# A hybrid retention and attention layer: tiles turned in 32x32 blocks on VectorE instead of on TensorE

## The chip, the cores and the metric

The kernel runs on one core of one Trainium2 chip. The metric is the device time of one execution, in microseconds (us). One core has TensorE (PE, with its weight loads as PEld), VectorE (DVE), ScalarE (ACT), GpSimd (POOL) and SyncE (SP, which here only issues transfers), and 16 DMA engines between DRAM and the on-chip memories.

## The reference

The layer takes x of 1024 tokens by 2048 features in float32, normalizes it, projects it to 6656 columns, runs two groups of heads, gates them, and projects back:

```python
h = rms_norm(x, norm_w)
rq, rk, rv, rg, aq, ak, av, ag = split(h @ w_in)
# group A: 8 retention heads x 128, chunks of 128 tokens, forward and backward
q, k = rotary(rq), rotary(rk) * 128**-0.5
inner = ((q @ k.T) * decay) @ v                 # inside a chunk
kv_chunk = k.T @ (k_dec * v)                    # one 128x128 state update per chunk and direction
cross = (q * q_dec) @ prev_state                # prev_state: scan over chunks, state * chunk_decay + kv_chunk
y = inner + cross                               # both directions added
y = (y - mean(y)) * rsqrt(var(y) + eps)         # per token and head
y_ret = (y * gn_w + gn_b) * silu(rg)
# group B: 8 query heads on 2 key/value heads, window of 128 tokens, partial rotary, a sink logit
y_att = windowed_softmax_attention(aq, ak, av, sink) * silu(ag)
x = x + concat(y_ret, y_att) @ w_out
return rms_norm(x, final_norm_w)
```

## The kernel before

The big products (x by w_in, and the gated outputs by w_out) are done in float32 precision as three passes each: an operand is split into a high and a low part (`split`, L84 and L87), and `mm3` (L98 to L100) issues high x high, high x low and low x high, each a 128x128 weight against 512 columns. Blocks of 2x2 tiles are combined in Strassen's manner into seven products. A product is four program steps, a step is six of these matmuls, and a unit of seven products is 28 steps. Every projected tile (52 of them, 128 features by 1024 tokens) is stored to a DRAM tensor `pr` by SP (first contribution) or added there by a POOL transfer (L258 to L262).

Attention, retention, gating and the weight loads run beside these products as generators: `advance()` is called once per step and moves each of them to its next `yield`; `idle(n)` passes n steps. So the program is written in one order, step by step. PE, SP and POOL execute it in that order. VectorE's and ScalarE's instructions are placed by a scheduler and then executed in that order. An instruction that waits holds up everything behind it on its engine or queue.

The tiles in `pr` have features on the partitions. Some steps need tokens there:

- Attention (L557): `take_v` turns the two v tiles (`ld`) by `transposed` (L537 to L543), which puts four 128x128 transposes on PE into one PSUM bank `ax`, and then splits the bank.
- A retention head (L772): it multiplies scores (L787), turns v with two groups of four transposes and copies them out on ScalarE (L797), waits until the head before is done (`busy`), turns k in the same way (L803), scales v on ScalarE (`vd`, L808), idles three steps, and then forms the outer products of `k_tok` and `vd` on PE (L820). A scan over chunks on VectorE (L832, L834) makes the states, and each state is split at once (L84, L87) into `sH` and `sL`, 128x128 at a time. Then come the inner and the cross products (L867, L854).
- `normed` (L880): mean and variance (L882, L883), the power on POOL (L888), eight VectorE instructions per head that normalize y (L891), two groups of four PE transposes, a ScalarE instruction on each bank that applies `gn_w` and `gn_b` (L899), and the store to the DRAM tensor `mix` by SP (L905). `k_tok` and `y` share a buffer.

While one head is computed, its successor's tiles are fetched by SP: kT and qT (L738), their halves exchanged for the rotary (`rx`, L744), and vT (L761). SP also issues the weight loads `a` (L171), each of which waits for the buffer that it fills: the last use of that buffer is a VectorE product `wL` (L84). The two weight buffers' contents are made two products ahead.

Gating (L1247) reads `mix` and the gate tiles back on ScalarE's queue, applies Silu and multiplies on VectorE.

## Time and profile before

| | |
|---|---|
| median of three runs | 1526.33 us (1524.84 to 1526.47) |
| span of the profiled execution | 1524.4 us |
| that execution's time around its span | the median is 1.9 us above the span |
| PE busy | 1510.5 us, 99% of the span |
| VectorE busy | 1088.3 us, 71% |
| ScalarE busy | 686.6 us, 45% |
| POOL busy | 151.0 us, 10% |
| granted TensorE clock | 0.9 or more in every slice |
| DMA | 153,352 packets, 310.53 MB, 204 GB/s on average |
| attention | about 230 to 690 us |
| retention | about 690 to 1115 us |
| gating and output product | from about 1115 us |

A row of the grouped view reads: line, engine, operation, output<-inputs, shapes, count | busy us, mean ns of one | idle time just before, and what ended it. A row of the timeline or of the chain of waits begins with its start and its duration in us. Rows with SPq are SP's issues of transfers, not the transfers. In the rows on DMA queues stand packets, megabytes and the share of 16 engines' time.

### The profile page before, as it was taken

The page shows a single profiled execution, that of the slowest core. Times are in us where ns is not written, and L with a number is a line of the kernel's source. Part 1 is how long each engine was busy: PE and PEld are TensorE (multiplying, and loading weights), DVE is VectorE, ACT ScalarE, POOL GpSimd, SP SyncE. Part 2 cuts the span into 40 slices and gives each one's busy share as a digit, 9 for nine tenths or more (in the row PEclk, how much of TensorE's full clock was granted, in tenths as well). Part 3 has the DMA queues.
Part 4 walks back from the last instruction along what each step waited for, and adds up shares of the span by engine and source line. Part 5 has one row for each costly group of instructions (what it writes and reads, how often), then busy time and mean ns, then how long its engine had stood idle before and what let it go on. Part 6 is the DMA issues. An engine that isn't in the chain of part 4 may idle for free.

```text
span 1524.4 us, 20497 instructions
## 1 busy us (share of the span) xinstructions
PE 1510.5 (99%) x7406; PEld 1274.0 (84%) x7406; DVE 1088.3 (71%) x1943; ACT 686.6 (45%) x1139; POOL 151.0 (10%) x169
## 2 busy tenths in 40 slices
PE   9999999999999999999999999999999999999997
PEld 7888888788888888888888888888888888888886
DVE  6896594557767575756977797779755966776766
ACT  7543462234545454533445444543444643542425
POOL 0000001111010000011212000001211102020001
PEclk9999999999999999999999999999999999999999
DMA  8288847889573424796677655488689679395756
GB/s 319 68 277 316 311 166 193 222 207 251 163 204 128 138 80 167 281 315 156 139 179 205 196 174 193 152 297 299 157 207 262 152 217 251 85 212 162 219 177 251
DMA packets 153352, 310.53 MB, mean 204 GB/s; under 512 B 13697, under 2 KB 72481, under 8 KB 144418
## 3 DMA queue, kind: packets, MB, share of 16 engines
q1 hardware_dynamic: 128050, 254.15, 49.1%
q0 software_dynamic: 19728, 36.71, 15.6%
q10 hardware_dynamic: 5472, 18.36, 3.5%
q8 instruction: 58, 0.95, 0.3%
q14 instruction: 44, 0.36, 0.1%
HBM read 193.03 MB, written 124.52 MB: 208 GB/s over the span
## 4 chain that ended last, share of the span: by engine, by line
PE 84%; issue 9%; DMA 4%; DVE 2%; POOL 0%; ACT 0%; SPq 0%; ACTq 0%; POOLq 0%; DVEq 0%
PE pj L100 21%; PE pj L98 21%; PE pj L99 21%; PE ax L99 5%; PE ax L100 5%; PE ax L98 5%; PE ax L820 2%; PE ax L542 1%; DMA xt<-in_x_dram 1%; PE ax L619 1%; DMA pr<-ct 1%; PE ax L787 1%; PE ax L867 1%; DMA yt<-pr 1%; DVE wL L84 0%
## 5 line engine op out<-in xcount | busy, mean ns | idle before, releaser
L98 PE MATMUL pj<-c,wH 128*128 128x512 f32 x1444 | 576.8, 399 | 0.0
L100 PE MATMUL pj<-c,wL 128*128 128x512 f32 x1440 | 562.6, 391 | 1.6 <-DVE wL L84 1.6
L99 PE MATMUL pj<-c,wH 128*128 128x512 f32 x1444 | 563.0, 390 | 0.0
L100 PEld LDWEIGHTS pj<-c,wL 128*128 128x128 f32 x1440 | 270.3, 188 | 60.7 <-DVE wL L84 2.5
L98 PEld LDWEIGHTS pj<-c,wH 128*128 128x128 f32 x1444 | 271.6, 188 | 49.7 <-ACT ct L292 0.4
L99 PEld LDWEIGHTS pj<-c,wH 128*128 128x128 f32 x1444 | 271.8, 188 | 49.5 <-DVE c L948 0.2
L87 ACT CAST wH<-a 128x1024 fp32r<-128x1024 f32 (+1 forms) x159 | 166.3, 1046 | 250.2 <-PE pj L99 138.0
L84 DVE TENSOR_TENSOR wL<-a,wH 128x1024 fp32r<-128x1024 f32 x157 | 191.9, 1222 | 109.4 <-ACT wH L87 105.9
L292 ACT COPY ct<-pj 128x512 f32<-128x512 f32 x192 | 111.1, 584 | 220.3 <-PE pj L100 219.7
L262 POOL DMA_DIRECT2D pr<-ct x104 | 92.2, 961 | 612.9 <-DVE ct L91 474.6
L91 DVE TENSOR_TENSOR ct<-pj,ct 128x512 f32<-128x512 f32 x164 | 109.1, 688 | 58.9 <-PE pj L100 58.0
L84 DVE TENSOR_TENSOR wL<-s,wH 128x1024 fp32r<-128x1024 f32 x56 | 68.4, 1222 | 89.8 <-ACT wH L87 89.4
L99 PE MATMUL pj<-wL,c 128*128 128x512 f32 x224 | 87.3, 390 | 0.0
L100 PE MATMUL pj<-wH,c 128*128 128x512 f32 x224 | 87.2, 389 | 0.0
L98 PE MATMUL pj<-wH,c 128*128 128x512 f32 x224 | 87.1, 389 | 0.0
L99 PE MATMUL ax<-wL,c 128*128 128x512 f32 x208 | 81.2, 390 | 0.4 <-DVE wL L84 0.4
L100 PE MATMUL ax<-wH,c 128*128 128x512 f32 x208 | 80.9, 389 | 0.0
L98 PE MATMUL ax<-wH,c 128*128 128x512 f32 x208 | 80.9, 389 | 0.0
L87 ACT CAST wH<-s 128x1024 fp32r<-128x1024 f32 x56 | 59.1, 1055 | 16.4 <-PE ax L100 8.8
L87 ACT CAST sH<-st 128x128 fp32r<-128x128 f32 x112 | 29.9, 298 | 46.9 <-DVE st L834 29.2
L99 PEld LDWEIGHTS pj<-wL,c 128*128 128x128 f32 x224 | 42.0, 188 | 8.9 <-DVE wL L84 0.3
L98 PEld LDWEIGHTS pj<-wH,c 128*128 128x128 f32 x224 | 42.0, 188 | 8.8
(243 smaller groups left out, 2057.7 us busy)
## 6 DMA issues: line engine op xcount, KB each, us to landing
a<-in_w_in_dram SPq DMA_DIRECT2D x103, 512.0 KB, 5.8
kept<-c SPq DMA_DIRECT2D x28, 1024.0 KB, 7.3
c<-kept SPq DMA_DIRECT2D x28, 1024.0 KB, 9.9
pr<-ct SPq DMA_DIRECT2D x110, 256.0 KB, 5.4
pr<-ct POOLq DMA_DIRECT2D x104, 256.0 KB, 6.2
a<-in_w_out_dram SPq DMA_DIRECT2D x18, 512.0 KB, 5.4
rx<-pr SPq DMA_DIRECT2D x64, 128.0 KB, 3.8
ysrc<-mix ACTq DMA_DIRECT2D x16, 512.0 KB, 5.4
```

The source lines that it names most:

```text
L84: return nc.vector.tensor_tensor(out=dst, in0=src, in1=high.bitcast(F32), op=ALU.subtract)
L87: behind(pinned, nc.scalar.copy(out=dst_h, in_=src))
L91: nc.vector.tensor_tensor(out=dst, in0=a, in1=b, op=ALU.add)
L98: nc.tensor.matmul(po, aH, bH, start=first, stop=False, **kw)
L99: nc.tensor.matmul(po, aH, bL, start=False, stop=False, **kw)
L100: nc.tensor.matmul(po, aL, bH, start=False, stop=last, **kw)
L262: nc.gpsimd.dma_start(out=dst, in_=t, accum_op=ALU.add)
L292: nc.scalar.copy(out=t, in_=bank)
L542: nc.tensor.transpose(pt[:, blk(t)], src[:, blk(b * 4 + t)], ident)
L619: nc.tensor.transpose(pt[:, blk(j)], s[:, blk(j)], ident)
L787: nc.tensor.matmul(sc[:, blk(t)], kT[:, c], qT[:, c], start=True, stop=True)
L820: nc.tensor.matmul(p, k_tok[:, c], vd[:, c, d], start=True, stop=True)
```

## The change

PE's 208 transposes of v, k and y go. VectorE's transpose instruction turns 32x32 blocks in place: a tile of 128x512 comes out with each of its 4x16 blocks turned, but with the blocks where they were. What is left, to put block (i, j) at (j, i), is done on the way through DRAM.

- The DRAM tensors of retention's v (8), attention's v (2), the first eight `mix`, and a new `kz` (8) become `blocked`: 8 chunks of 128x128. `gather` reads such a tensor with four transfers, each to 32 partitions and 32 runs of 32 floats (128 bytes) in each; `spot` and `like` give the places for the stores, whose runs become 512 bytes. An adding POOL store of a blocked tile becomes two.
- v is gathered (attention's on SP, retention's on SP), and VectorE turns the blocks after it.
- k is turned by VectorE after its rotary into two `ct`, stored to `kz`, and gathered into `k_tok` by SP after `idle(2)`; before the outer products stands `idle(4)` in place of `idle(3)`.
- y is normalized by 64 ScalarE instructions of 128x128 (scale and bias per token; the bias is one small VectorE instruction per head), turned by VectorE into two `ct`, and stored to `mix`; gating gathers it on ScalarE's queue and applies `gn_w` and `gn_b` there, one 128x1024 instruction per tile.
- The states' split is done for both directions at once, 256 columns in place of 128, with another order inside `sH` and `sL`.

```diff
+    def gather(q, dst, src):
+        of = src.rearrange("c (b j) (a t) -> a j (c b) t", j=SQ, t=SQ)
+        for a in range(P // SQ):
+            r = slice(a * SQ, (a + 1) * SQ)
+            q(out=dst[r].rearrange("p (n t) -> p n t", t=SQ), in_=of[a])
...
             def take_v():
-                for b, pt in transposed(kv["ldv"]):
-                    split(vH[:, 4 * b:4 * b + 4], vL[:, 4 * b:4 * b + 4], chunks(pt))
+                for b in range(2):
+                    z = ct()
+                    nc.vector.transpose(out=z, in_=kv["ldv"][:, half(b)])
+                    split(vH[:, 4 * b:4 * b + 4], vL[:, 4 * b:4 * b + 4], chunks(z))
...
                     add(u, u, b)
+                    if c == T_RK:
+                        zs.append(ct())
+                        nc.vector.transpose(out=zs[i], in_=u)
                     yield
                 kq[name, h] = t
+                for i, z in enumerate(zs):
+                    yield
+                    nc.sync.dma_start(out=spot(kz[h], i), in_=chunks(z))
...
-                nc.sync.dma_start(out=t, in_=pr[T_RV + h])
+                gather(nc.sync.dma_start, t, pr[T_RV + h])
...
-                for b, pt in transposed(vs.pop(h)):
-                    nc.scalar.copy(out=v[:, 4 * b:4 * b + 4], in_=chunks(pt))
+                vT = vs.pop(h)
+                for b in range(2):
+                    nc.vector.transpose(out=v[:, 4 * b:4 * b + 4], in_=chunks(vT[:, half(b)]))
                     yield
                 while busy:
                     yield
+                yield from idle(2)
                 k_tok = ret.tile([P, NT, P], F32, name="k_tok", tag="y")
-                for b, pt in transposed(kT):
-                    nc.scalar.copy(out=k_tok[:, 4 * b:4 * b + 4], in_=chunks(pt))
-                    yield
+                gather(nc.sync.dma_start, k_tok.rearrange("p c e -> p (c e)"), kz[h])
                 start(next_of("kT", T_RK, h + 1))
...
-                yield from idle(3)
+                yield from idle(4)
...
-                        split(sH[:, 2 * to + d - 1], sL[:, 2 * to + d - 1], cur[:, d])
                         if d == 1:
+                            both = slice(i, 2 * NT - 2 - i, 2 * NT - 3 - 2 * i)
+                            split(sH[:, both], sL[:, both], cur)
...
-                for c in range(NT):
-                    nc.vector.tensor_scalar(out=y[:, c], in0=y[:, c], scalar1=mv[:, c, 0:1], scalar2=rs[:, c:c + 1],
-                                            op0=ALU.subtract, op1=ALU.mult)
-                    if c % 4 == 3:
-                        yield
+                nc.vector.scalar_tensor_tensor(out=mv[:, :, 0], in0=mv[:, :, 0], scalar=-1.0, in1=rs, op0=ALU.mult, op1=ALU.mult)
+                zs = []
+                for b in range(2):
+                    for c in range(4 * b, 4 * b + 4):
+                        nc.scalar.activation(out=y[:, c], in_=y[:, c], func=AF.Identity, scale=rs[:, c:c + 1], bias=mv[:, c, 0:1])
+                    zs.append(ct())
+                    nc.vector.transpose(out=chunks(zs[b]), in_=y[:, 4 * b:4 * b + 4])
+                    yield
+                busy.discard(h)
                 yield from idle(2)
-                outs = []
-                for b, pt in transposed(y.rearrange("p c e -> p (c e)")):
-                    yo = ct()
-                    nc.scalar.activation(out=yo, in_=pt, func=AF.Identity, scale=gw[:, h:h + 1], bias=gb[:, h:h + 1])
-                    outs.append((mix[h][:, half(b)], yo))
-                    yield
-                busy.discard(h)
-                yield
-                for dst, yo in outs:
-                    nc.sync.dma_start(out=dst, in_=yo)
+                for b, z in enumerate(zs):
+                    nc.sync.dma_start(out=spot(mix[h], b), in_=chunks(z))
...
                 nc.scalar.activation(out=g, in_=g, func=AF.Silu)
+                if t < RH:
+                    nc.scalar.activation(out=d, in_=d, func=AF.Identity, scale=gw[:, t:t + 1], bias=gb[:, t:t + 1])
                 nc.vector.tensor_tensor(out=d, in0=d, in1=g, op=ALU.mult)
...
-                        behind(True, nc.scalar.dma_start(out=d, in_=mix[t]))
+                        if t < RH:
+                            gather(lambda **kw: behind(True, nc.scalar.dma_start(**kw)), d, mix[t])
+                        else:
+                            behind(True, nc.scalar.dma_start(out=d, in_=mix[t]))
```

The order of the instructions changes with it. In the listings below a line number belongs to the kernel that the listing is of; `mm3` moves from L98 to L100 to L99 to L101, and `split`'s subtraction from L84 to L85.

On PE, at the third head's v and k. `ax<-ident,vT` and `ax<-ident,kT` are the groups of four transposes. Before:

```order
L542 MATMUL ax<-ident,vT 128x128 x4
L98 MATMUL pj<-c_5644,wH 128x512
L99 MATMUL pj<-c_5644,wH 128x512
L100 MATMUL pj<-c_5644,wL 128x512
L98 MATMUL pj<-c_5644,wH 128x512
L99 MATMUL pj<-c_5644,wH 128x512
L100 MATMUL pj<-c_5644,wL 128x512
L542 MATMUL ax<-ident,kT 128x128 x4
```

and in the changed kernel, behind the scores:

```order
L817 MATMUL ax<-qT,kT 128x128 x4
L99 MATMUL pj<-c_5650,wH 128x512
L100 MATMUL pj<-c_5650,wH 128x512
L101 MATMUL pj<-c_5650,wL 128x512
L99 MATMUL pj<-c_5650,wH 128x512
L100 MATMUL pj<-c_5650,wH 128x512
L101 MATMUL pj<-c_5650,wL 128x512
```

The groups of transposes are gone, with nothing in their place on PE; only matmuls of the projection follow the scores.

On SP, at the fourth head. `a` is a weight tile, `pr` a projected tile, `res` a piece of x for the end, `mix` the head before's output. Before:

```order
L761 DMA vT<-pr_85 128x1024
L171 DMA a_8316<-in_w_in_dram 128x4x256
L260 DMA pr_113<-ct 128x512
L260 DMA pr_114<-ct 128x512
L171 DMA a_8371<-in_w_in_dram 128x4x256
L171 DMA a_8373<-in_w_in_dram 128x4x256
L905 DMA mix_120<-ct 128x512 x2
L1153 DMA res_246<-in_x_dram 16x16384
L738 DMA kT<-pr_78 128x1024
L744 DMA rx<-pr_78 64x512 x4
L171 DMA a_8493<-in_w_in_dram 128x4x256
```

and in the changed kernel:

```order
L164 DMA vT<-pr_85 32x32x32 x4
L284 DMA pr_113<-ct 128x512
L284 DMA pr_114<-ct 128x512
L195 DMA a_8268<-in_w_in_dram 128x4x256
L195 DMA a_8270<-in_w_in_dram 128x4x256
L1180 DMA res_254<-in_x_dram 16x16384
L932 DMA mix_120<-ct 128x4x128 x2
L195 DMA a_8362<-in_w_in_dram 128x4x256
L164 DMA k_tok<-kz_137 32x32x32 x4
L762 DMA kT<-pr_78 128x1024
L768 DMA rx<-pr_78 64x512 x4
```

The gather of `k_tok` now stands on SP directly behind a weight load, `a_8362`, and ahead of the next head's kT and `rx`; the outer products on PE need it four program steps later.

On VectorE, in attention, at its first rotary. `rx` are the exchanged halves, `wL` a weight's low part, `ct` an evicted product. Before:

```order
L84 TENSOR_TENSOR wL<-s_2217,wH 128x1024
L94 TENSOR_TENSOR s_2217<-a_2073,s_2217 128x1024
L526 TENSOR_TENSOR rx_2287<-rx_2287,rt_2283 64x512
L91 TENSOR_TENSOR ct<-pj,ct 128x512 x2
L84 TENSOR_TENSOR wL<-a_2033,wH 128x1024
L526 TENSOR_TENSOR rx_2288<-rx_2288,rt_2284 64x512
```

and in the changed kernel:

```order
L85 TENSOR_TENSOR wL<-s_2227,wH 128x1024
L95 TENSOR_TENSOR s_2227<-a_2081,s_2227 128x1024
L92 TENSOR_TENSOR ct<-pj,ct 128x512 x2
L85 TENSOR_TENSOR wL<-a_2041,wH 128x1024
L85 TENSOR_TENSOR wL<-a_2079,wH 128x1024
L553 TENSOR_TENSOR rx_2302<-rx_2302,rt_2298 64x512
```

The eviction of a product and two low parts of weights now stand ahead of the rotary's product; before, they stood behind it.

More of the change, by code (lines that the diff above doesn't have):

```diff
@@ L19 @@
 P = 128
+SQ = 32
 S = 1024
@@ L136, in together, with blocked, spot, like @@
             yield
-    pr = [dram.tile([P, S], F32, name=f"pr{i}") for i in range(52)]
-    mix = [dram.tile([P, S], F32, name=f"mix{i}") for i in range(KT)]
+    BLOCKED = [*range(T_RV, T_RV + RH), T_AV, T_AV + 1]
+    def blocked(name):
+        return dram.tile([NT, P, P], F32, name=name)
+    pr = [blocked(f"pr{i}") if i in BLOCKED else dram.tile([P, S], F32, name=f"pr{i}") for i in range(52)]
+    mix = [blocked(f"mix{i}") if i < RH else dram.tile([P, S], F32, name=f"mix{i}") for i in range(KT)]
+    kz = [blocked(f"kz{i}") for i in range(RH)]
+    def spot(t, m):
+        if len(t.shape) == 2:
+            return t[:, half(m)]
+        return t[4 * m:4 * m + 4].rearrange("c p f -> p c f")
+    def like(t, ap):
+        return t if len(ap.shape) == 2 else chunks(t)
+    def gather(q, dst, src):
[3 more added lines that the diff above has]
+            q(out=dst[r].rearrange("p (n t) -> p n t", t=SQ), in_=of[a])
     rows_d = dram.tile([1, HALF], F32, name="rows_d")
@@ L259, in flush @@
             if first:
-                nc.sync.dma_start(out=dst, in_=t)
-            else:
-                nc.gpsimd.dma_start(out=dst, in_=t, accum_op=ALU.add)
+                nc.sync.dma_start(out=dst, in_=like(t, dst))
+            elif len(dst.shape) == 2:
+                nc.gpsimd.dma_start(out=dst, in_=t, accum_op=ALU.add)
+            else:
+                for c in range(0, 4, 2):
+                    nc.gpsimd.dma_start(out=dst[:, c:c + 2], in_=chunks(t)[:, c:c + 2], accum_op=ALU.add)
         stores.clear()
@@ L267, in store @@
         def store(n, m, t):
-            stores.append((True, pr[BLOCKS[b] // P + 2 * n + a][:, half(m)], t))
+            stores.append((True, spot(pr[BLOCKS[b] // P + 2 * n + a], m), t))
         if i == 1:
@@ L287, in store @@
         def store(n, m, t):
-            stores.append((b not in seen, pr[BLOCKS[b] // P + 2 * n + a][:, half(m)], t))
+            stores.append((b not in seen, spot(pr[BLOCKS[b] // P + 2 * n + a], m), t))
         if i in (1, 6, 5, 4):
@@ L535, in rotate_att @@
         return rotate(pool, rot_a, [([(c, 0, 32) for c in tiles], [(c, r, 16) for c in tiles for r in (16, 0)]) for tiles in sets])
-    def transposed(src):
-        for b in range(2):
-            pt = ax()
-            for t in range(4):
-                nc.tensor.transpose(pt[:, blk(t)], src[:, blk(b * 4 + t)], ident)
-            yield b, pt
     clock = [0]
@@ L566, in fetch @@
                 kv[n] = att.tile([P, S], F32, name="ld", bufs=2)
-                nc.sync.dma_start(out=kv[n], in_=pr[c])
+                if n == "ldv":
+                    gather(nc.sync.dma_start, kv[n], pr[c])
+                else:
+                    nc.sync.dma_start(out=kv[n], in_=pr[c])
             def take_k():
@@ L738, in fetch @@
                 nc.sync.dma_start(out=t, in_=pr[c + h])
-                beside = []
+                beside, zs = [], []
                 def pair(i):
@@ L1043, in scale_first @@
             for e, of in zip(es, unscaled[i:i + 2]):
-                nc.sync.dma_start(out=e, in_=of)
+                nc.sync.dma_start(out=like(e, of), in_=of)
             yield from idle(8)
```

11 lines of the change are left out of this document (6 added, 5 removed).

## The prediction

> **What bounds the kernel now.** First the page: share of the span by engine, and the chain that ended last. Then the window of retention, where 48 of the 52 groups of transposes stand.
>
> ```profile
> span 1524.4 us, 20497 instructions
> PE 1510.5 (99%) x7406; PEld 1274.0 (84%) x7406; DVE 1088.3 (71%) x1943; ACT 686.6 (45%) x1139; POOL 151.0 (10%) x169
> PE 84%; issue 9%; DMA 4%; DVE 2%; POOL 0%; ACT 0%; SPq 0%; ACTq 0%; POOLq 0%; DVEq 0%
> 690.00:1115.00 425.00, 424.88 (x2297) 364.58 (x2296) 331.92 (x771) 189.26 (x336) 52.06 (x44) 1.00 0.67 192
> ```
>
> PE sets the end: it is busy for 424.88 of 425 us in retention, and the chain runs through it. VectorE (331.92) has 93 us free there and ScalarE (189.26) 236 us, so work that leaves PE for them shortens the span, as long as nothing that PE waits for comes later.
>
> Next, what a group of four transposes costs in the chain, and how many there are.
>
> ```profile
> 710.35 0.23 PE pj L100
> 710.58 0.44 PE ax L542 x4
> 711.01 0.23 PE pj L98
> ...
> L542 PE MATMUL ax<-ident,y 128*128 128x128 f32 x64 | 9.6, 272 | 0.0
> L542 PE MATMUL ax<-ident,vT 128*128 128x128 f32 x64 | 9.6, 272 | 0.0
> L542 PE MATMUL ax<-ident,kT 128*128 128x128 f32 x64 | 9.6, 272 | 0.0
> L542 PE MATMUL ax<-ident,ld 128*128 128x128 f32 x16 | 2.4, 271 | 0.0
> ```
>
> A group holds the chain for 0.44 us (a matmul of 512 columns for 0.23). The means of 272 ns overlap each other, so the chain is the row to count by.
>
> **The change part by part.** *PE.* 3 x 64 + 16 = 208 transposes are 52 groups: 52 x 0.44 = **-22.9 us**. No matmul is added.
>
> *One stall less.* In attention PE waits once for a weight whose product stands on VectorE behind a rotary that waits for its transfer:
>
> ```profile
> 272.42 3.28 DMA rx<-pr
> ...
> 276.09 0.67 DVE ct L91
> 276.76 1.14 DVE wL L84
> 277.91 0.04 issue
> 277.95 0.50 PE pj L100
> ```
>
> In the new order that eviction and that `wL` stand ahead of the rotary. PE's L100 takes 0.50 in the chain and waits besides; the gap that closes is about 1 us: **-1**. From below 0, if the rotary's wait falls on the next row that PE needs.
>
> *VectorE.* A transpose of 128x512 isn't in this trace. The nearest rows of that shape:
>
> ```profile
> L467 DVE TENSOR_SCALAR xp<-xp,rms 128x512 f32<-128x512 f32 x16 | 7.1, 485 | 1.8 <-DMA xp<-in_x_dram 1.7
> L91 DVE TENSOR_TENSOR ct<-pj,ct 128x512 f32<-128x512 f32 x164 | 109.1, 688 | 58.9 <-PE pj L100 58.0
> L956 DVE TENSOR_SCALAR src<-ax,vec_t 128x512 f32<-128x512 f32 x4 | 3.0, 745 | 0.0
> L891 DVE TENSOR_SCALAR y<-y,mv,rstd 128x128 f32<-128x128 f32 x64 | 18.4, 342 | 5.0 <-POOL rstd L888 5.0
> L84 DVE TENSOR_TENSOR sL<-st,sH 128x128 fp32r<-128x128 f32 x112 | 28.3, 288 | 0.4 <-ACT sH L87 0.3
> L84 DVE TENSOR_TENSOR qbL<-q,qbH 128x256 fp32r<-128x256 f32 x32 | 13.1, 416 | 8.8 <-ACT qbH L87 8.8
> ```
>
> Between 485 and 745 ns; I take 690, the row with the most instructions, to be careful. 48 of them in retention add 33 us (23 to 36). The normalization of y leaves (-18.4), and 112 splits of 128 columns become 56 of 256 (56 x 0.416 = 23.3 against 28.3: -5). Net +10 us on 332 busy of 425: beside PE, at no cost to the end as long as each single wait stays short. If that cover were gone, the price is the 10 us.
>
> *ScalarE.* The three groups of rows that read the turned banks go, and 64 activations of 128x128 come:
>
> ```profile
> L797 ACT COPY v_tok<-ax 128x512 f32<-128x512 f32 x16 | 9.4, 587 | 14.3 <-PE ax L542 14.3
> L803 ACT COPY k_tok<-ax 128x512 f32<-128x512 f32 x16 | 9.6, 600 | 0.0
> L899 ACT ACTIVATE ct<-ax,vec_t 128x512 f32<-128x512 f32 x16 | 12.5, 782 | 13.6 <-PE ax L542 13.6
> L776 ACT ACTIVATE dT<-dT 128x128 f32<-128x128 f32 x8 | 2.5, 310 | 8.8 <-DVE dT L775 8.8
> ```
>
> -31.5 + 64 x 0.31 = 19.8 gives -12 us in retention. In gating 8 activations of about 1.1 us and 24 more issues stand on an engine that is 45% busy: hidden. POOL's 20 more adding transfers stand on an engine with 10%. In-order waits on these engines can still reach PE now and then; I put **+2** (0 to 6) for them: gating begins 5 steps later, and its first operand is then ready 7 steps (9.6 us) ahead of its use in place of 12, so most of that is covered.
>
> *The gathers.* They are the price. What is late next is `k_tok`: before, it came from PE and ScalarE with nothing between; now it is stored, gathered, and needed by the outer products four steps after the gather. Its landing time L has a fixed part and a part by runs.
>
> ```profile
> rx<-pr SPq DMA_DIRECT2D x64, 128.0 KB, 3.8
> 869.05 2.39 SPq L744 DMA_DIRECT2D rx<-pr  x4
> ...
> q1 hardware_dynamic: 128050, 254.15, 49.1%
> ...
> q10 hardware_dynamic: 5472, 18.36, 3.5%
> ...
> DMA packets 232, 0.09 MB, mean 226 GB/s; under 512 B 173, under 2 KB 228, under 8 KB 228
> q1 hardware_dynamic: 232, 0.09, 81.4%
> ...
> DMA packets 520, 0.52 MB, mean 259 GB/s; under 512 B 15, under 2 KB 520, under 8 KB 520
> q1 hardware_dynamic: 520, 0.52, 84.8%
> ```
>
> (The two last pairs are DMA windows: 176.6 to 177.0 us, mostly packets under 512 bytes, and 861 to 863 us, packets of 1 KB.) By engine and packet, q10 takes 0.035 x 16 x 1524.4 / 5472 = 156 ns for 3355 bytes and q1 0.491 x 16 x 1524.4 / 128050 = 94 ns for 1985 bytes: a line of 0.046 ns per byte and 3 ns. A run of 128 bytes would be 9 ns by it. The small packets of the first window took 0.4 x 16 x 0.814 / 232 = 22 ns. So 9 to 22 ns; I take 13, since the line carries thousands of packets and the window holds some larger ones. A gather is 4 x 1024 runs, 256 on each of 16 engines: 3.3 us (2.3 to 5.6). The fixed part is rx's 3.8 less its own bytes, 8 KB on an engine or 0.4 us: 3.4 to 3.5 us. Four issues take 2.4 us and run beside it, so at the lower end 6.0 rather than 5.8. **L = 6.8 us, 6.0 to 9.1.**
>
> Against it stands the time from the gather's issue to its use. The gather follows a weight load on SP, and that load waits for a buffer. At the fourth head:
>
> ```profile
> 872.60 0.39 PE L98 MATMUL pj<-c,wH 128*128 128x512 f32 x1
> 873.96 1.06 PE L820 MATMUL ax<-vd,k_tok 128*128 128x128 f32 x8
> 875.78 0.39 SPq L171 DMA_DIRECT2D a<-in_w_in_dram  x1
> ```
>
> The load's step begins on PE at 872.60 (its six matmuls end where L820 begins, so a step is 1.37 us) and the load is issued at 875.78, 3.2 us later; with its own 0.39 it holds the queue for 3.6 us. A head's program is 29 steps long now (28 before: 8 in place of 7 between the v transposes' start and the outer products), the weights' unit still 28, so the gather drifts by one step per head against the loads. Counted in the program, from the last load ahead of it to the outer products there are 10, 11 or 12 steps at the first three heads (outside trouble), then 5, 6, 7, 8, 9. Time left is steps x 1.37 - 3.6: 3.2, 4.6, 6.0, 7.4, 8.7 us. At the fourth head v's two transposes now stand on VectorE ahead of the `wL` that frees the buffer, 1.4 us, of which 0.6 replaces kT's rotary there: 2.4 in place of 3.2. Against 6.8 the stalls are 4.4, 2.2, 0.8, 0, 0, and 1 more where the seventh head's gather shares the queue with two kept operands of 1 MB: **+8.4 us** (+5 at L = 6.0; +17 at 9.1). The gathers of v have five idle steps and those of attention have longer; they add nothing at this L.
>
> Sum: -22.9 - 1 + 8.4 + 2 = -13.5 on the profiled 1524.4, or 1510.9. The median of the runs stands 1.9 above the span: **1513 us**. Its own range, from +5 and 0 to +17 and +6, is 1507 to 1526.
>
> **The rivals.**
>
> *B, the gathers come in time.* The 3.2 us of the load's wait came behind evictions that stand elsewhere in the new order; where the load goes out at its step's beginning, 3.2 us come back at each head and only the fourth waits a little. Then 1524.4 - 23.9 + 1 to 2, plus 1.9: **1504**. For it: VectorE has time. Against it: the new order has the `wL` in the same place.
>
> *C, a run costs twice.* 26 ns in place of 13: L = 3.5 + 6.7 = 10.2, the stalls 7.8, 5.6, 4.2, 2.8, 1.5 and 1, together 23. 1524.4 - 23.9 + 23 + 2 + 1.9 = **1527**, no change. For it: 22 ns in the window of small packets. Against it: that window's packets aren't all small.
> The Trainium skill's page "DMA: Bandwidth & Descriptors", section "Specifications", has a rule that speaks for this case: below 512 bytes a DMA engine reads, modifies and writes. By that rule the runs of 128 bytes would cost like twice their number; the 22 ns row leaves room for it, the line through the large packets doesn't show it.
>
> *D, a run costs as much as a packet of 1 KB* (the other side). In the second window it is 2 x 16 x 0.848 / 520 = 52 ns. If a run's price is by its number and not by its bytes, a gather takes 13.3 + 3.5 = 16.8 us: the last five heads wait for 14.4, 12.2, 10.8, 9.4 and 8.1 us (55), the first three (10.1, 11.5 and 12.8 left) for 16. 1524.4 - 23.9 + 71 + 2 + 1.9 = **1575**. It decides from 26 ns per run, where the stalls eat the gain. Against it: q10's 3355 bytes at 156 ns and 1 KB at 52 ns go with the bytes.
>
> *E, VectorE's queue holds PE up.* A transpose waits for its gather or its y at the head of an in-order queue, with evictions (L91) and low parts of weights behind it. If all 52 x 0.69 = 36 us came through to PE: 1524.4 - 23.9 + 36 + 8.4 + 1.9 = **1547**. It decides where a transpose waits longer than the 11.6 us that VectorE has free per head (93 / 8). Against it: the five steps ahead of v's transposes are 6.9 us, L's own size.
>
> *F, no gain*, that PE's groups filled time in which it would have waited: the chain's rows at 710 us show matmuls at 0.23 us on both sides, without a wait.
>
> **How the numbers follow.** The forecast 0.48, B 0.20, C 0.13, D 0.12, E 0.05, F 0.02. A measurement of this kernel tells about 0.2% (3 us) from no change. The forecast gives faster almost whole, B whole, C half of its 0.13 to no change and the rest to both sides: faster 0.71, within 0.2% 0.09, slower 0.20. The range reaches from B's lower side to a little past C: 1501 to 1532; D and E lie outside.
>
> **What would show it.** PE's instructions on L542's places gone and 0.23 us on both sides of them: the first term. Waits of PE on `k_tok` at its outer products: about 4, 2 and 1 us at the fourth to sixth head and none at the first three; waits at all eight are D, none is B. The gather's median to landing at 6 to 9 us; the transposes' mean at 485 to 745 ns. VectorE's busy time in retention's window at about 342 us. I am wrong if PE waits for VectorE behind a transpose, if v's gathers are late too, or if gating opens with a gap.

## The result, and the profile after

The changed kernel takes 1616.22 us (median of 4 runs, 1609.2 to 1618.83) against 1525.77 us before: a ratio of 1.0587 with a 95% interval of 1.0564 to 1.0611. It is 90 us slower, where 13 us less had been forecast and a range of 1501 to 1532 given.

The page of the changed kernel, and from its view of waits what PE waited for, in us in total, times, and the longest:

```profile
span 1613.8 us, 20192 instructions
PE 1519.7 (94%) x7198; PEld 1270.9 (79%) x7198; DVE 1105.4 (69%) x1883; ACT 682.3 (42%) x1107; POOL 182.1 (11%) x189
...
PE ax L850 <- DMA k_tok<-kz: 25.5, 5, 9.9
PE ax L817 <- DVE qT L92: 16.3, 1, 16.3
PE pj L99 <- ACT ct L319: 11.4, 3, 5.8
PE ax L99 <- ACT y L899: 7.2, 1, 7.2
PE pj L99 <- ACT wH L88: 6.2, 3, 3.1
PE ax L99 <- ACT wH L88: 4.2, 2, 3.9
```

The transposes are gone (7198 matmuls, 208 fewer), but PE is idle for 94.1 us of the span, 13.9 before. That is 80 of the 89.4 us by which the span grew. The other 9 are in PE's busy time, which rose from 1510.5 to 1519.7 although the transposes, 22.9 us by the prediction's price, had left it.

Three of these waits (16.3, 11.4 and 7.2 us) have no gather in their names. All three lead to POOL, as the runs below bear out. This is POOL's timeline at the third head; a row ends with the idle time ahead of it and its releaser:

```profile
883.18 1.20 POOL L289 DMA_DIRECT2D pr<-ct  x1 [2.38 <-issue]
887.64 1.23 POOL L289 DMA_DIRECT2D pr<-ct  x1 [3.26 <-issue]
891.54 1.21 POOL L289 DMA_DIRECT2D pr<-ct  x1 [2.67 <-issue]
895.36 1.23 POOL L289 DMA_DIRECT2D pr<-ct  x1 [2.61 <-issue]
899.23 1.21 POOL L289 DMA_DIRECT2D pr<-ct  x1 [2.64 <-issue]
900.00 2.14 POOL L919 TENSOR_TENSOR rstd<-rstd,neg_half 128x8 f32<-128x8 f32 x1
```

Every adding store to a blocked tile is issued 3.8 to 4.5 us after the one ahead of it here, though the profile shows no instruction that it waits for ("issue"). In the trace each goes out 0.3 us after its predecessor has landed: the store of 891.54 lands at 895.04 and the next one starts at 895.36. Before, an adding store was one transfer of 128 runs (a run is a piece that lies together in DRAM; a blocked tile now takes two transfers of 256 runs in its place), and two went out back to back in 1.78 us:

```profile
684.69 1.78 POOL L262 DMA_DIRECT2D pr<-ct  x2 [3.69 <-DVE ct L91]
...
POOL pr L262 <- issue: 8.0, 4, 3.4
```

In the changed kernel the same view reads:

```profile
POOL pr L289 <- issue: 115.6, 31, 8.4
```

Behind this queue two things are late. One is the power for `rstd` (L919): it stands on POOL behind 16 such stores, VectorE's next instruction waits for it, and the rotary of q stands behind that on VectorE. The waits from 850 to 910 us:

```profile
ACT y L925 <- DVE mv L921: 24.8, 1, 24.8
DVE mv L921 <- POOL rstd L919: 19.5, 1, 19.5
PE ax L817 <- DVE qT L92: 16.3, 1, 16.3
ACT ct L319 <- DMA pr<-ct: 11.9, 1, 11.9
```

The other is the buffers `ct`: a store that is not yet issued holds its buffer, so ScalarE's eviction waits for `pr<-ct` (11.9 us in the last row), and PE for the bank.

### The profile page after: what moved, and what is told of

It is laid out like the page before. It is cut to its first block, busy times and chain, and to the rows that moved or that the text cites. A ratio compares the mean times of both kernels' runs of the same rounds, so it can differ in the third digit from the quotient of the medians.

```text
span 1613.8 us, 20192 instructions
## 1 busy us (share of the span) xinstructions
PE 1519.7 (94%) x7198; PEld 1270.9 (79%) x7198; DVE 1105.4 (69%) x1883; ACT 682.3 (42%) x1107; POOL 182.1 (11%) x189
## 5 line engine op out<-in xcount | busy, mean ns | idle before, releaser
L99 PE MATMUL pj<-c,wH 128*128 128x512 f32 x1444 | 580.3, 402 | 12.1 <-ACT ct L319 11.4
L101 PE MATMUL pj<-c,wL 128*128 128x512 f32 x1440 | 567.6, 394 | 4.1 <-DVE wL L85 4.1
L100 PE MATMUL pj<-c,wH 128*128 128x512 f32 x1444 | 568.7, 394 | 0.0
L99 PEld LDWEIGHTS pj<-c,wH 128*128 128x128 f32 x1444 | 275.4, 191 | 65.4 <-ACT ct L319 12.7
L101 PEld LDWEIGHTS pj<-c,wL 128*128 128x128 f32 x1440 | 273.8, 190 | 65.6 <-DVE wL L85 6.5
L100 PEld LDWEIGHTS pj<-c,wH 128*128 128x128 f32 x1444 | 275.4, 191 | 51.8 <-DVE c L975 0.2
L85 DVE TENSOR_TENSOR wL<-a,wH 128x1024 fp32r<-128x1024 f32 x157 | 191.6, 1221 | 120.4 <-ACT wH L88 117.9
L286 POOL DMA_DIRECT2D pr<-ct x84 | 75.8, 961 | 517.3 <-DVE ct L92 428.8
L85 DVE TENSOR_TENSOR wL<-s,wH 128x1024 fp32r<-128x1024 f32 x56 | 68.4, 1221 | 55.9 <-ACT wH L88 55.6
L99 PE MATMUL pj<-wH,c 128*128 128x512 f32 x224 | 89.1, 398 | 5.5 <-ACT wH L88 5.5
L100 PE MATMUL pj<-wL,c 128*128 128x512 f32 x224 | 89.5, 400 | 2.3 <-DVE wL L85 2.3
L101 PE MATMUL pj<-wH,c 128*128 128x512 f32 x224 | 88.7, 396 | 0.0
L99 PE MATMUL ax<-wH,c 128*128 128x512 f32 x208 | 81.9, 394 | 4.2 <-ACT wH L88 4.2
L100 PE MATMUL ax<-wL,c 128*128 128x512 f32 x208 | 82.0, 394 | 1.4 <-DVE wL L85 1.4
L101 PE MATMUL ax<-wH,c 128*128 128x512 f32 x208 | 81.5, 392 | 0.0
L289 POOL DMA_DIRECT2D pr<-ct x40 | 48.5, 1212 | 165.3 <-issue 115.6
L850 PE MATMUL ax<-vd,k_tok 128*128 128x128 f32 x224 | 34.5, 300 | 25.6 <-DMA k_tok<-kz 25.5
L850 PEld LDWEIGHTS ax<-vd,k_tok 128*128 128x128 f32 x224 | 33.3, 213 | 30.4 <-issue 27.9
```

The costliest lines, as they stand in the source:

```text
L85: return nc.vector.tensor_tensor(out=dst, in0=src, in1=high.bitcast(F32), op=ALU.subtract)
L99: nc.tensor.matmul(po, aH, bH, start=first, stop=False, **kw)
L100: nc.tensor.matmul(po, aH, bL, start=False, stop=False, **kw)
L101: nc.tensor.matmul(po, aL, bH, start=False, stop=last, **kw)
L286: nc.gpsimd.dma_start(out=dst, in_=t, accum_op=ALU.add)
L289: nc.gpsimd.dma_start(out=dst[:, c:c + 2], in_=chunks(t)[:, c:c + 2], accum_op=ALU.add)
```

## The experiments

**POOL's queue alone.** First the layout without anything else:

```diff
-    pr = [dram.tile([P, S], F32, name=f"pr{i}") for i in range(52)]
+    pr = [blocked(f"pr{i}") if i in BLOCKED else dram.tile([P, S], F32, name=f"pr{i}") for i in range(52)]
...
+            elif len(dst.shape) == 2:
+                nc.gpsimd.dma_start(out=dst, in_=t, accum_op=ALU.add)
             else:
-                nc.gpsimd.dma_start(out=dst, in_=t, accum_op=ALU.add)
+                for c in range(0, 4, 2):
+                    nc.gpsimd.dma_start(out=dst[:, c:c + 2], in_=chunks(t)[:, c:c + 2], accum_op=ALU.add)
...
```

> The kernel before with one part of the change alone: the projected tiles of v (retention's eight, attention's two) become blocked tensors, so that their adding POOL stores go out as 20 pairs of 128x2x128 in place of 20 of 128x512, and their other stores and loads move in runs of 512 bytes. Nothing is gathered or turned by VectorE; the transposes stay on PE. Theory P (a POOL transfer of 256 runs waits until the one ahead of it has landed): 20 to 45 us slower than before, 1547 to 1572, with PE waiting for evictions (ct) and for what stands behind the power on POOL. Rival (POOL's stores cost only in company with the gathers, which keep the DMA engines busy): within 8 us of 1526.

Measured: 1572.74 us against 1526.03, ratio 1.0309 (1.0294 to 1.0324). With PE doing all its transposes, no gather in the kernel, and VectorE unchanged, half of the loss is there. PE's waits and POOL's:

```profile
PE ax L564 <- DVE y L913: 16.0, 1, 16.0
PE pj L98 <- DVE ct L91: 12.4, 1, 12.4
PE ax L564 <- DMA vT<-pr: 8.5, 1, 8.5
...
POOL pr L284 <- issue: 90.2, 28, 6.7
```

It is the same chain: the 16.0 us are y's transposes, behind VectorE's normalization of y, which waits 21.1 us for the power that POOL begins at 898 us. The rival, that these stores cost only in company with the gathers, falls.

Then the other way round, the change with smaller stores:

```diff
-                for c in range(0, 4, 2):
-                    nc.gpsimd.dma_start(out=dst[:, c:c + 2], in_=chunks(t)[:, c:c + 2], accum_op=ALU.add)
+                for c in range(4):
+                    nc.gpsimd.dma_start(out=dst[:, c:c + 1], in_=chunks(t)[:, c:c + 1], accum_op=ALU.add)
```

> The changed kernel with one edit: an adding POOL store of a blocked tile goes out as four transfers of 128x1x128 (128 runs of 512 bytes each) in place of two of 128x2x128 (256 runs each). Theory P (POOL's queue): a transfer of 256 runs isn't issued before the one ahead of it has landed (3.6 us from issue to issue in the changed kernel's trace), so POOL runs late, evictions find no free ct, and the power for rstd stands behind it; 128 runs were issued back to back in the kernel before (0.87 us each). P expects POOL's 80 small stores back to back at about 0.9 us, PE's waits on ct (11.4 us), on y's copy (7.2) and on qT (16.3) gone, and with them the slower clock behind them: 1616 falls to 1560 to 1575. The waits on k_tok (25.5) and those in gating (some 14) stay. Rival R (the gathers load the DMA engines, and POOL's stores are late like all others): the stores land no sooner, within 10 us of 1616; rival B (the 512-byte runs of the stores are dear by number): also no gain, since the number of runs is the same.

Measured: 1577.43 us, ratio 1.0331 (1.0316 to 1.0347) to the kernel before: 39 us less than the change, a little short of the 41 to 56 expected. POOL's timeline shows that these stores wait too:

```profile
692.52 2.66 POOL L289 DMA_DIRECT2D pr<-ct  x3 [3.69 <-DVE kT L775]
695.95 2.68 POOL L289 DMA_DIRECT2D pr<-ct  x3 [0.76 <-issue]
698.98 0.87 POOL L289 DMA_DIRECT2D pr<-ct  x1 [0.35 <-issue]
701.27 2.65 POOL L289 DMA_DIRECT2D pr<-ct  x3 [1.43 <-issue]
```

Transfers of 128 runs go out about three at a time at 0.88 us each and then wait too; those of 256 runs go one at a time. So it is the number of runs on their way in this queue that is bounded, not bytes: 80 transfers of 64 KB do better than 40 of 128 KB, and before, up to three of 256 KB were on their way together. By the times of issue and landing no trace of this case has more than 384 runs there at once: three stores of 128, or one of 256 with one of 128, never two of 256. The expectation's "back to back" held only for the first three; the waits on `ct` and y's copy went, and 5.0 us of the 16.3 on qT stayed.

**v kept in rows.** The same gather can be read from a row-major tile with one more dimension in the pattern, so that the blocked layout isn't needed:

```diff
-    pr = [blocked(f"pr{i}") if i in BLOCKED else dram.tile([P, S], F32, name=f"pr{i}") for i in range(52)]
+    pr = [dram.tile([P, S], F32, name=f"pr{i}") for i in range(52)]
...
+        if len(src.shape) == 2:
+            of = src.rearrange("(b j) (c a t) -> a j c b t", a=P // SQ, j=SQ, t=SQ)
+            for a in range(P // SQ):
+                r = slice(a * SQ, (a + 1) * SQ)
+                q(out=dst[r].rearrange("p (c b t) -> p c b t", b=P // SQ, t=SQ), in_=of[a])
+            return
```

> The changed kernel with one edit: the projected tiles of v stay as rows of 1024 tokens, stored and added whole as before (104 adding POOL stores of 128x512, 2 KB runs), and v's gathers read the same 128-byte runs from those rows by a pattern with one more dimension. The gathers keep number and size of their runs; k and y are as in the changed kernel. Theory P: all POOL waits on a landing go, as in the run with four parts, 1555 to 1570. Rival R (the gathers' load): nothing changes, 1605 to 1620. If the pattern itself were slow, v's gathers would land later than their 4.5 us median and VectorE would wait for them at v's transposes.

Measured: 1566.31 us, ratio 1.026 (1.024 to 1.028): 50 us less than the change. The median from issue to landing of v's gathers is 4.2 us here and 4.5 in the change: the pattern costs nothing that the median shows. Theory P stands. What is left over the kernel before is 40 us, and PE's waits name it:

```profile
PE ax L856 <- DMA k_tok<-kz: 27.1, 5, 11.1
PE ax L99 <- ACT wH L88: 5.0, 2, 4.1
PE pj L99 <- ACT wH L88: 4.2, 3, 1.6
```

**k.** Of this kernel, k alone goes back to PE (two groups of transposes and ScalarE's copies, no `kz`, and three idle steps behind them in place of two ahead and four behind):

```diff
-                yield from idle(2)
...
-                gather(nc.sync.dma_start, k_tok.rearrange("p c e -> p (c e)"), kz[h])
+                for b, pt in transposed(kT):
+                    nc.scalar.copy(out=k_tok[:, 4 * b:4 * b + 4], in_=chunks(pt))
+                    yield
...
-                yield from idle(4)
+                yield from idle(3)
```

> The run with v kept in rows, and k turned on PE and copied by ScalarE as before (no kz, no gather of k_tok, three idle steps ahead of the outer products); v and y as in the change. It gives back 16 x 0.44 = 7 us of transposes to PE and takes the waits on k_tok (27.1 us in that run) with the slower clock behind them. Theory: 1566 + 7 - 27 - 5 = 1541, 1536 to 1546, the rest over 1517 being gating's. Rival (the waits on k_tok only show lateness that has its cause elsewhere, and PE will wait at the next place): over 1555.

Measured: 1536.01 us, ratio 1.0066 (1.0043 to 1.0089): 30 us less, where 25 were expected. k's part gives PE 7 us of transposes and takes 37. How much of that comes from the gather's place in the program is shown by the run with the gather two steps earlier:

```diff
-                yield from idle(2)
                 k_tok = ret.tile([P, NT, P], F32, name="k_tok", tag="y")
...
-                yield from idle(4)
+                yield from idle(6)
```

> The run with v kept in rows with one other edit: k_tok's gather is issued two steps earlier in the head's program (the idle of two steps ahead of it goes behind it: six steps from the gather to the outer products in place of four, the head's length unchanged). At the fourth head it now stands ahead of the weight load that it stood behind. Theory (the prediction's): the wait at the outer products is L minus the time left; with 2.7 us more at each head and without the load ahead at the fourth, the waits of 4.0, 2.8 and 2.3 us at heads four to six go, and of 10.1 and 7.0 at the seventh and eighth some 7 to 11 us together stay: 12 to 18 us less than the run before. Rival: the queue is full there because of the kept operands of 1 MB, and an earlier gather only waits longer in SP's queue: under 6 us.

Measured: 1549.04 us, ratio 1.0144 (1.0127 to 1.0161), 17 us less, as the theory had it. PE's waits on k_tok fall from 27.1 to 16.5 us; those of the fourth and fifth head are gone, 1.8 us stay at the sixth, and 7.0 and 7.1 us at the seventh and eighth. These two are another matter, seen in the change's SP timeline. The fourth head first, then the seventh; the second number is the time that SP spent on the issues:

```profile
918.85 0.37 SPq L195 DMA_DIRECT2D a<-in_w_in_dram  x1
919.27 3.69 SPq L164 DMA_DIRECT2D k_tok<-kz  x4
...
1074.24 3.98 SPq L1136 DMA_DIRECT2D c<-kept  x1
1078.32 0.51 SPq L195 DMA_DIRECT2D a<-in_w_in_dram  x1
1078.92 0.68 SPq L1136 DMA_DIRECT2D c<-kept  x1
1079.65 2.56 SPq L284 DMA_DIRECT2D pr<-ct  x2
1082.25 11.03 SPq L164 DMA_DIRECT2D k_tok<-kz  x4
```

Four issues take 3.69 us when the queue is nearly empty, and 11.03 us behind loads of 1 MB and stores: SP itself is held. From the first issue to the last landing it is 6.9 us at the fourth head (the prediction's L was 6.8) and 14.1 and 17.1 us at the seventh and eighth.

**The blocks put in place at the store.** If a gather is dear where someone waits for it, the small runs can stand at the store:

```diff
+    def scatter(q, dst, src, n):
+        to = dst.rearrange("c (a t) (b j) -> b t (c a) j", t=SQ, j=SQ)
+        for b in range(P // SQ):
+            q(out=to[b][:, 16 * n:16 * n + 16], in_=src[b * SQ:(b + 1) * SQ].rearrange("p (n j) -> p n j", j=SQ))
...
```

> The run with k_tok's gather two steps earlier and v kept in rows, with the blocks of k and y put in place where they are stored, not where they are loaded: eight stores per head and tensor of 32 partitions and 16 runs of 128 bytes, and then one load per tile in runs of 512 bytes (k_tok on SP, mix on ScalarE's queue). The number of 128-byte runs stays, but none stands between a load's issue and its use. Theory (what is dear is the landing and the issue of the gathers in places where PE or ScalarE wait for them): the waits on k_tok (16.5 us) fall under 6, those in gating (about 12) under 3: 1549 falls to 1515 to 1530. Rival (the runs of 128 bytes load all queues, wherever they stand): over 1540.

Measured: 1539.01 us, ratio 1.0086 (1.0071 to 1.0101): 10 us less, not the 19 to 34 expected. The theory's half on gating held: the waits on `wH` there are no longer among PE's larger ones. Its half on k did not:

```profile
PE ax L864 <- DMA k_tok<-kz: 12.4, 3, 10.6
PE pj L100 <- DMA c<-kept: 3.9, 1, 3.9
...
1016.34 11.30 SPq L163 DMA_DIRECT2D mix<-ct  x8
```

One wait of 10.6 us at the seventh head stays although `k_tok` is now one transfer: eight stores of y's blocks hold SP for 11.30 us, and `k_tok`'s load is issued at 1028.72, behind them. The kept operands, whose loads stand there too, are late themselves. Around the last two heads this queue has no room for the 4096 runs of such a tile without delay, wherever they stand. So the time lies beside the rival's bound of 1540, not in the theory's range.

**Gating.** ScalarE issues the gathers of `mix` itself. Its timeline in the change:

```profile
1299.19 7.32 ACTq L1310 DMA_DIRECT2D ysrc<-mix  x4
1306.60 1.89 ACTq L1313 DMA_DIRECT2D yt<-pr  x1
1308.53 1.05 ACT L88 CAST wH<-a 128x1024 fp32r<-128x1024 f32 x1 [8.32 <-DMA ysrc<-mix]
```

Five issues take 9.2 us of ScalarE, and the cast that PE needs stands behind them. Moving those gathers to SP, with v in rows:

```diff
-                            gather(lambda **kw: behind(True, nc.scalar.dma_start(**kw)), d, mix[t])
+                            gather(nc.sync.dma_start, d, mix[t])
```

> The run before (v kept in rows) with one more edit: gating's gathers of mix are issued by SP in place of ScalarE's queue, the gate tiles stay on ScalarE's. Theory: in the changed kernel an issue of such a gather takes 1.6 to 4.4 us of ScalarE where the queues are full, and ScalarE's casts, which PE waits for, stand behind it (ScalarE waited 44.6 us on its own transfers in 1290 to 1390 us). Expected: those waits fall under 10 us, PE's waits for wH and wL in gating (about 14 us) fall under 4, time 10 to 18 us below the run before. Rival: it is the landing that is late, not the issue; then the gains stay under 4 us, and the waits move to SP's weight loads, which now stand behind the gathers.

Measured: 1561.69 us, ratio 1.0228 (1.0212 to 1.0243), 4.6 us less, where the theory had 10 to 18. ScalarE's casts no longer stand behind its own issues, but PE's waits in gating become one of 11.2 us, because a weight load stands behind four issues on SP:

```profile
1317.52 11.30 SPq L170 DMA_DIRECT2D ysrc<-mix  x4
1328.91 0.51 SPq L1199 DMA_DIRECT2D s<-in_w_out_dram  x1
```

Of the 11.30 us three issues took 6.9, and the fourth stood 4.1 more until a transfer of `yt` had landed. So theory and rival each had a part: the issue does hold ScalarE, but moved to SP it holds the weight loads.

**The parts that move no tile through DRAM** (y normalized on ScalarE, `gn_w` and `gn_b` in gating, the merged split), alone on the kernel before:

```diff
-                    nc.vector.tensor_scalar(out=y[:, c], in0=y[:, c], scalar1=mv[:, c, 0:1], scalar2=rs[:, c:c + 1],
-                                            op0=ALU.subtract, op1=ALU.mult)
+                    nc.scalar.activation(out=y[:, c], in_=y[:, c], func=AF.Identity, scale=rs[:, c:c + 1], bias=mv[:, c, 0:1])
...
-                    nc.scalar.activation(out=yo, in_=pt, func=AF.Identity, scale=gw[:, h:h + 1], bias=gb[:, h:h + 1])
+                    nc.scalar.copy(out=yo, in_=pt)
...
+                if t < RH:
+                    nc.scalar.activation(out=d, in_=d, func=AF.Identity, scale=gw[:, t:t + 1], bias=gb[:, t:t + 1])
```

> The kernel before with the parts of the change that move no tile through DRAM: y normalized on ScalarE (64 activations, the small bias on VectorE), gn_w and gn_b applied in gating, the states' split merged to 256 columns. All transposes stay on PE; ScalarE's instruction on y's turned banks becomes a plain copy. Theory (what y's part costs, 11 us between the run of v alone and the run with k on PE, is the gathers of mix on ScalarE's queue and the stores): within 3 us of 1526. Rival (the longer way of gating through ScalarE, or the merged split, costs it): 1532 or more.

Measured: 1528.9 us, ratio 1.0021 (1.0011 to 1.0031): 2.5 us slower, inside the theory's bound.

**v alone on the kernel before**, from rows:

```diff
-                nc.sync.dma_start(out=t, in_=pr[T_RV + h])
+                gather(nc.sync.dma_start, t, pr[T_RV + h])
...
-                for b, pt in transposed(vs.pop(h)):
-                    nc.scalar.copy(out=v[:, 4 * b:4 * b + 4], in_=chunks(pt))
+                vT = vs.pop(h)
+                for b in range(2):
+                    nc.vector.transpose(out=v[:, 4 * b:4 * b + 4], in_=chunks(vT[:, half(b)]))
                     yield
```

(and the same for attention's `ld` in `take_v`).

> The kernel before with one part of the change alone, in the form of the run with v kept in rows: v is gathered from row-major tiles and turned by VectorE, for retention and for attention; k and y stay on PE and everything else as before. 20 of the 52 groups of PE's transposes go, 20 x 0.44 = 8.8 us. Theory (v's gathers have five steps to land and cost PE nothing): 1516 to 1520. Rival (VectorE's in-order queue or the gathers' place on SP cost more than they give): 1526 or more.

Measured: 1524.91 us, ratio 0.9995 (0.9986 to 1.0005): no gain, where 8.8 us were expected. PE's busy time did fall, from 1510.5 to 1503.2 us, but PE is idle for 19.2 us, 13.9 before. Its waits show where: 3.8 us at the last head on `vd`, whose v stood on VectorE behind an eviction, and in attention small ones on ScalarE and VectorE of 1.0, 0.8 and 0.3 us. Two repairs of that, attention's v back on PE and three more idle steps for the last head:

```diff
-                yield from idle(3)
+                yield from idle(3 if h < RH - 1 else 6)
```

> The kernel before with retention's v alone gathered from rows and turned by VectorE (attention's v stays on PE), and six idle steps in place of three ahead of the outer products of the last head alone, where VectorE's transposes of v stood behind an eviction in the run of v alone and PE waited 3.8 us for vd. 16 groups of transposes go: -7.0 us. Theory (v's part is free of cost where its transposes have time): 1518 to 1521. Rival (the gathers or VectorE's queue cost as much at places that the waits of the run of v alone did not show): 1524 or more.

Measured: 1523.54 us, ratio 0.9986 (0.9977 to 0.9996). That is 0.14% faster, under the 0.2% that counts here, and short of the 7 us. The waits have moved (the profile is of the slowest of the 11 executions, 1527.98 us):

```profile
PE pj L100 <- DMA c<-kept: 3.2, 1, 3.2
...
1043.33 11.92 SPq L148 DMA_DIRECT2D vT<-pr  x4
1055.30 2.77 SPq L1118 DMA_DIRECT2D c<-kept  x1
```

v's gather holds SP for 11.92 us in the stretch of the kept loads, and in this execution a kept load is late. Adding y's part to it, with the blocks put in place at the store:

```diff
-                    nc.sync.dma_start(out=spot(mix[h], b), in_=chunks(z))
+                    scatter(nc.sync.dma_start, mix[h], z, b)
...
-                            gather(lambda **kw: behind(True, nc.scalar.dma_start(**kw)), d, mix[t])
+                            behind(True, nc.scalar.dma_start(out=chunks(d), in_=by_chunk(mix[t])))
```

> The run of retention's v alone, with y's part of the change too: y normalized on ScalarE, turned by VectorE, its blocks put in place at the store (32 partitions, 16 runs of 128 bytes), mix loaded in one transfer per tile on ScalarE's queue, gn_w and gn_b in the gating, and the states' split merged. k stays on PE. Another 16 groups go: -7 on the run of v alone. Theory (gating's price was the gathers on ScalarE's queue): 1511 to 1517. Rival (gn_w and gn_b in the gating, or the 16 stores of 512 runs per engine queue, cost as much): 1520 or more.

Measured: 1543.89 us, ratio 1.0108 (1.0092 to 1.0123), 20 us slower than v alone and well past the rival's bound of 1520. `gn_w` and `gn_b` in the gating and the merged split cost only the 2.5 us above. That stores of small runs are the rest is what remains, but no run took them alone: PE waited 6.5 us at the last head's scores, and in 15 places, 3.4 us at most, for weights. Why this is 8 us worse than the run with y's gathers in gating (1536.01) was not settled.

The steps from kernel to kernel, each one part of the change more, by the medians:

| kernel | us | step |
|---|---|---|
| before | 1526.0 | |
| v from rows | 1524.9 | -1.1 |
| and y, gating, split | 1536.0 | +11.1 |
| and k | 1566.3 | +30.3 |
| and v's tensors blocked: the change | 1616.2 | +49.9 |

In the rounds of these runs the kernel before had medians of 1525.8 to 1526.5 us, so the first step is no difference. The steps hold for this order; the last part alone on the kernel before cost 46.7 us.

## Why the prediction was wrong

**"POOL's 20 more adding transfers stand on an engine with 10%"** is the step that failed first: 50 of the 90 us. The engine's busy share says nothing of a queue that lets only so many runs be on their way. The prediction counted 20 more transfers, and not that each now had 256 runs. The trace before has only transfers of 128 runs, but it does show that the queue is bounded: 45 of its 136 adding stores went out as the third under way and none as a fourth, and four waited on "issue", 8.0 us in all.

```profile
260.30 0.86 POOL L262 DMA_DIRECT2D pr<-ct  x1 [3.57 <-ACT ct L292]
264.57 0.88 POOL L262 DMA_DIRECT2D pr<-ct  x1 [3.41 <-issue]
```

The second of these goes out 0.31 us after the landing of the oldest of three. Whether transfers, runs or bytes are counted can't be told from this trace, so a store of twice as many runs was a form of unknown price and should have had an upper end: 40 transfers with a landing each, at the 6.2 us to landing of the page before, are an estimated 248 us of POOL, with `ct` and the power behind them. No rival had it.

**The gathers.** The price of a run was right. The trace holds the time of each packet: those of 128 bytes took 13 ns in the median, and in the mean 14.7 on SP's queue and 16.0 on ScalarE's (9 to 22 had been given, 13 taken). The page of the profile agrees: ScalarE's queue took 0.035 x 16 x 1524.4 = 854 us of engine time before and 0.047 x 16 x 1613.8 = 1214 after, for 32128 more packets and the same bytes, so that a packet more costs 11 ns, to which the time of its 128 bytes comes:

```profile
q10 hardware_dynamic: 37600, 18.36, 4.7%
```

So rival D, which came out nearest in time (1575), had the wrong cause, and rival C too: 26 and 52 ns are refuted. The Trainium skill's rule that below 512 bytes a DMA engine reads, modifies and writes ("DMA: Bandwidth & Descriptors", section "Specifications") doesn't show in this price: packets of 512 bytes, 1, 2 and 4 KB took 27, 46, 84 and 159 ns in the median, and the line through them gives 13 ns at 128 bytes. L was right where the queue was quiet: 6.9 us and a wait of 3.9 at the fourth head, against 6.8 and 4.4. The fifth and sixth waited 2.6 and 2.2 (2.2 and 0.8 forecast), and the first three not at all, as forecast. The term that was mis-sized is "1 more where the seventh head's gather shares the queue with two kept operands": it was 9.9 us there and 6.9 at the eighth, where none was forecast. L was taken as one number, but the issue itself stretches when the queue is full.

**ScalarE and gating at +2.** The 24 more issues were taken as hidden. An issue on ScalarE's queue that takes 0.33 us early in gating takes up to 4.3 later, and it is ScalarE's own time. In the run with k on PE, PE's waits behind 1200 us come to 12.4 us (0.4 before), so most of y's step of 11.1 us lies there; no run took the gathers of `mix` alone.

**A term that was missing: the clock behind a wait.** The prediction counted a wait at its own length. After the 16.3 us wait PE's matmuls read:

```profile
904.82 2.04 PE L817 MATMUL ax<-qT,kT 128*128 128x128 f32 x8 [16.29 <-DVE qT L92]
907.57 0.80 PE L99 MATMUL pj<-c,wH 128*128 128x512 f32 x1 [0.70 <-ACT wH L88]
...
911.13 0.63 PE L100 MATMUL pj<-c,wH 128*128 128x512 f32 x1
911.56 0.63 PE L101 MATMUL pj<-c,wL 128*128 128x512 f32 x1
...
912.66 0.40 PE L101 MATMUL pj<-c,wL 128*128 128x512 f32 x1
912.89 0.39 PE L99 MATMUL pj<-c,wH 128*128 128x512 f32 x1
```

From 904.7 to 911.5 the granted clock was 0.50, and matmuls start every 0.43 us in place of 0.23. In sum PE's busy time should have fallen by 22.9 us and rose by 9.2, so about 32 us are work at a lower rate. The granted clock accounts for most of it: 14 stretches of the trace were at 0.50, with PE busy for 57.4 us in them, of which half, 28.7, would not have been needed at the full clock. In the trace before, no stretch at half clock is recorded while PE was busy. The Trainium skill's page "TensorE: Matmul & The Clock Gate", in its part 1, gives half rate after an idle window and full rate after a busy window of some 3.4 us, and has these windows run freely. This trace agrees: the stretches lasted 3.4 us or 2, 3 and 6 times that. The one here ended 7.5 us after the first matmul, with one more gap of 0.7 us in between.

**What held.** The transposes' price: less the time lost at half clock, PE's busy time is 1491.0 us in the change, 19.5 less than before (22.9 forecast), and with v alone 1501.6, 8.9 less for 20 groups (8.8 forecast). VectorE's transpose took 690 to 709 ns (690 taken), and VectorE was 69% busy: it had the time, as argued, and rival E came only in the small (the 3.8 us on `vd` with v alone). ScalarE's activations on y took 483 ns in place of 310, 25.9 us in place of 19.8, with room beside PE. The stall in attention, "one stall less", didn't go but grew: PE waited 3.1 us for `wL` at 290.8 us. With the layout alone it waited 12.4 us for an eviction at that place, and with v in rows that stall is absent (PE has no gap over 0.2 us between 78 and 440 us), so the -1 holds where POOL's stores of attention's v aren't in the way.

## What to carry to other kernels

When a layout changes, count the runs of every transfer that touches it, not only of the new ones, and look in the trace for how many are ever on their way together: a queue that lets a bounded number of runs be on their way turns a 10% busy engine into the one that all wait for. A transfer's price has three parts, the landing, the issue, and what the full queue adds to the issue; the last is paid by the engine that issues, so small runs belong to a queue and a stretch in which nothing that PE needs stands behind them. And a wait that PE can't hide costs more than its length, since the matmuls behind it start at half the clock.

## What the runs showed of the hardware that was not expected

- Adding stores from POOL: no trace has more than 384 runs on their way there. Transfers of 256 runs (128 partitions, runs of 512 bytes) were issued one at a time, nearly all 0.3 us after the landing of the one before, which made 3.6 to 9.7 us from issue to issue in the change, 4.2 in the median; transfers of 128 runs went up to three at a time at 0.88 us.
- Four issues of 1024 runs took 2.2 to 3.7 us of the issuing engine in a quiet queue. In the change they took up to 12.6 us on SP, where loads of 1 MB were under way, and up to 9.7 on ScalarE.
- Runs of 128 bytes from DRAM took 13 ns each of a DMA engine in the median, on the line through packets of 512 bytes to 4 KB.
- A wait of 2.6 us on PE (to 980.0 us) was followed by 3.4 us at half clock, one of 2.2 us (to 1033.3) was not.
- A pattern of four dimensions for a gather (32 partitions, 8 chunks, 4 blocks, 32 floats) landed as fast as one of three: 4.2 against 4.5 us in the median.
